# Retention state updates in four row groups of 32 tokens, and four feed-forward weight blocks in two column parts

## The chip, the cores and the metric

The kernel runs on one core of one Trainium2 chip, in one launch. The metric is the device time of that launch in microseconds (us). Before the change it is 1624.82 us, the median of 3 runs (1624.66 to 1625.16). TensorE (PE) does the matrix products, VectorE (DVE), ScalarE (ACT) and GpSimd (POOL) the rest, and SyncE (SP) issues nearly all of the DMA transfers.

## The reference

One layer of a hybrid decoder, for 256 prompt tokens and 8 sample sequences of 8 tokens (320 tokens in all), with a model width of 2048:

```
mod = silu(c) @ w_ada + b_ada                      # six modulation vectors per sequence
h   = rmsnorm(x, g_pre_mix) * (1 + sc1) + sh1
q, k, v, g, u, vs = split(h @ w_in)                # 48 tiles of 128 features
q, k = rotary(q), rotary(k) * 128 ** -0.5
o, S = retention(q, k, v, s0)                      # 8 heads of 128
m   = concat(silu(g) * layernorm(o), gelu(u) * spatial_gate(layernorm(gelu(vs)))) @ w_o
x   = x + gt1 * rmsnorm(m, g_post_mix)
f   = square(relu((rmsnorm(x, g_pre_ffn) * (1 + sc2) + sh2) @ w_ff1)) @ w_ff2
x   = x + gt2 * rmsnorm(f, g_post_ffn)
```

In the retention, each head of each sample sequence has a state of 128 x 128, and the layer returns the new one: `S_new = S * gamma**8 + sum over the 8 tokens of gamma**(7-s) * k_s^T v_s`. That is 8 heads x 8 sequences = 64 products over 8 tokens each.

## The kernel before

Features lie on the partitions and the 320 tokens on the free axis. Each weight block of 128 x 128 is split into a high and a low part (ACT's cast at L234, DVE's subtraction at L110), each activation tile too, and a product is three matmuls of 320 columns into one accumulator: high x high, high x low, low x high (`mm3`, L243 to L245). These 9216 matmuls are the bulk of PE's work; below they are the main matmuls. Weights come in pieces of 1 MB through four raw buffers; the adaLN weights (`adaw`) share those buffers, and their small matmuls (L187, here "ada rows", four of which run in the four column groups of the array) are strewn between the others.

The input projection runs over K in slices of 1, 1, 2, 4 and 8 blocks. In the last slice (8 blocks, 24 main matmuls per tile of 128 features) the finished tiles go straight into the mixers: after tile 7 the spatial gate's norm (`sgu`), and after every sixth tile from 13 on one call of `ret_pair` for two heads (four calls, here the first to the fourth pair). Such a call does, for each of its two heads: rotary on q and k (`rot`: four ACT copies into `sw` and six DVE products and sums), transposes of v and k on PE (`pv`, `pk`, L412 to L420), scores (`sc`, L426 to L428), masked scores on DVE (`sT`, `s_pad`, with the mask `dm` loaded by DMA at L406), and outputs (`po`, L437 to L444, the last eight of which read the old states `s0`, loaded at L404). The sample tokens of the two heads lie on partitions 0 to 63 and 64 to 127 of `vts` and `kts`.

Then, once per pair, the state update: POOL makes, for two sequences at a time, `ve`, a copy of `vts` for each of the two in which the rows of other sequences are zero and the others carry the decay (`bm` holds these factors); PE multiplies `kts` with it, one product of 64 rows and 256 columns per head (`pn`, L465, from the pool of three small PSUM buffers); DVE adds the result to the decayed old state (L470) and SP stores it (L471).

The order of instructions on each engine is not the source's. The framework's scheduler orders them by source position and by its own estimate of when operands and buffers come free, so work of the next tiles is placed between the steps of a pair where it fits. Each engine then runs its list strictly in that order, and so does SP with the DMA issues. PSUM has eight buffers of one bank: four accumulators (`new_acc`), three small ones (`small`) and one for the ada rows. `NSLOT` is the number of SBUF slots of 128 x 320 from which nearly all tiles come, `ve` among them.

Of the kernel before, what the change touches and what calls it, by code (L numbers as in the profile page):

```python
# [26 lines left out]
EPS = 1e-6  # L27
NSLOT = 104
NRAW = 4
# [23 lines left out]
def _per_piece(ci):  # L53
    """Column tiles in a piece of w_in for slice ci of K."""
    return 8 if ci == 0 else 16 // CHUNKS[ci]


def _w_in_pieces():
    """Pieces of w_in in load order: (K blocks, column tiles)."""
    out, k0 = [], 0  # L60
    for ci, kc in enumerate(CHUNKS):
        nt = _per_piece(ci)
        for q in range(0, ZT, nt):
            out.append((list(range(k0, k0 + kc)), N_ORDER[q : q + nt]))
        k0 += kc
    return out + [(list(range(KB)), [t]) for t in G_ORDER]


def _ada_groups():
    """Groups of w_ada columns (feature tiles of 128) in load order, by the part that they serve."""  # L70
    pre, k0 = [], 0
    for kc in CHUNKS:
        if kc == 1:
            pre.append([KB + k0, k0])
        else:
            pre += [[KB + k, KB + k + 1, k, k + 1] for k in range(k0, k0 + kc, 2)]
        k0 += kc
    gt1 = [[2 * KB + 4 * q + j for j in range(4)] for q in range(4)]
    ffn = [[4 * KB + k, 4 * KB + k + 1, 3 * KB + k, 3 * KB + k + 1] for k in range(0, KB, 2)]
    gt2 = [[5 * KB + 4 * q + j for j in range(4)] for q in range(4)]  # L80
    return pre, gt1, ffn, gt2
# [3 lines left out]
def hybrid_step(ctx: ExitStack, tc, A, O):  # L85
# [15 lines left out]
    def slot(s="z", dt=F32, shape=(P, T)):  # L101
        return slots.tile(list(shape), dt, tag="slot", name=nm(s))
# [14 lines left out]

# [1 line left out]
    eps = cp.tile([P, 1], F32, name="eps")  # L119
# [16 lines left out]
    crs = cst[:, 288:352].rearrange("p (h s) -> p h s", h=H)  # L136
    bm = cst[:, 352:384].rearrange("p (q b) -> p q b", q=4)
    bada = vec[:, 0:96]
# [10 lines left out]
    def rsqrt_(out, var, n):  # L149
        """out = 1/sqrt(var + EPS); var [P, n]."""  # L150
        y, a = [slot("rq") if n == T else tp.tile([P, n], F32, tag=f"rq{n}", name=nm("rq")) for _ in range(2)]
        S.activation(y, var, AF.Abs_reciprocal_sqrt, bias=eps)
        V.scalar_tensor_tensor(out=a, in0=y, scalar=-0.5, in1=y, op0=ALU.mult, op1=ALU.mult)
        V.scalar_tensor_tensor(out=a, in0=var, scalar=EPS, in1=a, op0=ALU.add, op1=ALU.mult)
        V.scalar_tensor_tensor(out=out, in0=a, scalar=1.5, in1=y, op0=ALU.add, op1=ALU.mult)
# [4 lines left out]
    def mean_rsqrt(parts, pm=None):  # L160
        """[P, T] squares (any number of parts) -> 1/sqrt(mean + EPS) on every partition."""
        if pm is None:
# [6 lines left out]

# [1 line left out]
    ada_piece = [0]  # L171

    def ada_group(feats):
        """Generator: one step per 1 MB piece; feats are feature tiles 0..95."""
        ncol = P * len(feats)
# [46 lines left out]

# [1 line left out]
    def load_w(src, ncol=KB, eng=None):  # L224
        """A piece of ncol 128x128 blocks; returns the (high, low) pair of each block."""
        w = wp.tile([P, 2048], F32, tag="raw", bufs=NRAW, name=nm("raw"))
# [13 lines left out]
    def mm3(acc, w, a, start, stop):  # L240
# [4 lines left out]
        PE.matmul(acc[:, :T], wl, ah, start=False, stop=stop)  # L245

    def new_acc():
        return ps_acc.tile([P, 512], F32, tag="acc", name=nm("acc"))
# [7 lines left out]
    def modulate(xt, r, Am, Sm, f, eng=None):  # L256
        """xt*A*r + shift, as a high and a low part; A and shift per feature and sequence."""
        t = slot("mt")
# [12 lines left out]

# [1 line left out]
    k0s = [sum(CHUNKS[:i]) for i in range(len(CHUNKS))]  # L273
# [20 lines left out]

# [1 line left out]
    gateT = [None] * 8  # L296
# [72 lines left out]

# [1 line left out]
    def rot(q):  # L371
# [7 lines left out]
    oT = [None] * 8  # L379
    # sample tokens on partitions: sequence b = 4i + j, step s at row 32j + 8i + s, other rows zero  # L380
    q_pad = [cp.tile([P, 272], F32, name=f"q_pad{i}") for i in range(2)]
# [10 lines left out]
    def ret_pair(qkv, pr, o, mv):  # L392
        """Heads 2*pr and 2*pr+1: scores, states, token-major outputs and their statistics."""
        kts, vts = slot("kts"), slot("vts")
        os_ = slot("os")
        s0s, qs = [], []
        for e in range(2):
# [59 lines left out]
            s0s.append(s0)  # L457
        for i in range(4):
            ve = slot("ve")
            tt(ve[:, :256].rearrange("p (b e) -> p b e", b=2), vts[:, :128].unsqueeze(1).broadcast_to([P, 2, P]),  # L460
               bm[:, pr, 2 * i : 2 * i + 2].unsqueeze(2).broadcast_to([P, 2, P]), ALU.mult, G)
            pns = [small("pn") for _ in range(2)]
            for e in range(2):
                rw = slice(64 * e, 64 * e + 64)
                PE.matmul(pns[e][:, :256], kts[rw, :128], ve[rw, :256], start=True, stop=True)  # L465
            for e in range(2):
                h = 2 * pr + e
                g8 = float((1.0 - 2.0 ** (-5.0 - h)) ** NS)
                sb = s0s[e][i][:, :256]
                V.scalar_tensor_tensor(out=sb, in0=sb, scalar=g8, in1=pns[e][:, :256], op0=ALU.mult, op1=ALU.add)  # L470
                nc.sync.dma_start(O["ss"][h, i], sb)  # L471
        return os_
# [27 lines left out]

# [1 line left out]
    z = {}  # L502
# [82 lines left out]

# [1 line left out]
    for gi, f in enumerate(G_ORDER):  # L587
# [7 lines left out]

# [1 line left out]
    def project(name, base, n, act, order, first4, extra, done, w0=None):  # L597
        """n tiles of 128 outputs, contraction over act; done(m, acc) takes each."""
        m = 0
        while m < n:  # L600
# [16 lines left out]
            for i in range(KB):  # L617
                k = order[i]
                mm3(acc, w[k], act[k], i == 0, i == KB - 1)
            done(m, acc)  # L620
# [6 lines left out]
    def add_sq(key, src, final):  # L627
        """Squares of a tile; all but the final one are summed first."""
        sq = slot("sq")
# [22 lines left out]
    project("w_o", 0, KB, mix, ks_o, True, lambda: steps(ada_b, EXTRA_O), done_o)  # L652
# [1 line left out]
    w0 = load_w(A["w_ff1"][0])  # L654
# [23 lines left out]

# [1 line left out]
    facc = [None] * KB  # L680
# [31 lines left out]
def _consts():  # L712
# [27 lines left out]
    for pr in range(4):  # L740
        for b in range(NB):
            for e in range(2):
                col = np.where(sb == b, gam[2 * pr + e] ** (NS - 1.0 - ss), 0.0) * sc
                cst[64 * e : 64 * e + 64, 352 + 8 * pr + b] = col

# [90 lines left out]
```

## Time and profile before

| | |
|---|---|
| median of 3 runs | 1624.82 us |
| profiled execution: span | 1622.0 us |
| profiled execution's own time beside its span | the page gives the span only; the median of the runs lies 2.8 us above it |
| PE busy | 1567.2 us, 97% of the span |
| DVE busy | 822.3 us, 51% |
| ACT busy | 577.3 us, 36% |
| POOL busy | 260.8 us, 16% |
| four pairs of `ret_pair` | between about 262 and 417 us from the start |

A busy share is an average over stages. A row of the timeline gives the start, the length, the engine, the line and operation, what is written from what, and in brackets the engine's idle time just before with what ended it. `x16` stands for 16 instructions in one row. A float32 product takes two passes through the array, so it shows as two matmuls and two weight loads.

### The profile page before, as it was taken

Reading aid. Unit: us, or ns where it says so; the run is one execution under the profiler, and the core shown is the slowest. Engines: PE = TensorE matmul, PEld = TensorE weight load, DVE = VectorE, ACT = ScalarE, POOL = GpSimd, SP = SyncE. Lnnn points to the kernel's source line nnn. Section 1 sums busy time; section 2 is a strip of 40 time slices with the busy share of each in tenths; the row PEclk is TensorE's granted clock in tenths of the full one; section 3 lists DMA queues with packets and bytes.
Section 4 is the critical chain, followed back from the end, with each engine's and each line's share of the span. In section 5 each row is a group of like instructions: output and inputs, shape, how many; then the busy total and the mean of one; then the engine's idle time right before and its main releaser. Section 6 shows DMA issues by size and latency. Waiting matters only on the chain.

```text
span 1622.0 us, 25797 instructions
## 1 busy us (share of the span) xinstructions
PE 1567.2 (97%) x10744; PEld 1437.5 (89%) x10744; DVE 822.3 (51%) x1306; ACT 577.3 (36%) x847; POOL 260.8 (16%) x287
## 2 busy tenths in 40 slices
PE   4999998999999999899999999999999999999994
PEld 3788887888788888588899999999999999999994
DVE  5676658576744444863433344444444444444455
ACT  3523234233433323343333334332344323343331
POOL 2510016000000111621100022100121000211222
PEclk8999999999999999999999999999999999999997
DMA  6777785556566776766644444443444344444421
GB/s 244 282 290 300 314 321 194 199 212 228 203 253 256 284 278 257 278 244 249 253 155 156 145 143 155 156 148 140 155 156 150 140 152 157 154 139 150 156 104 65
DMA packets 63620, 325.03 MB, mean 200 GB/s; under 512 B 7152, under 2 KB 26096, under 8 KB 27024
## 3 DMA queue, kind: packets, MB, share of 16 engines
q1 hardware_dynamic: 61680, 320.89, 53.6%
q8 instruction: 84, 1.38, 0.4%
q10 hardware_dynamic: 1584, 1.68, 0.3%
q0 software_dynamic: 240, 0.82, 0.1%
q14 instruction: 32, 0.26, 0.0%
HBM read 315.76 MB, written 7.60 MB: 199 GB/s over the span
## 4 chain that ended last, share of the span: by engine, by line
PE 92%; DVE 5%; ACT 1%; DMA 1%; issue 1%; POOL 0%; SPq 0%; DVEq 0%; POOLq 0%
PE acc L243 28%; PE acc L245 27%; PE acc L244 27%; PE ada L187 6%; DVE gm L110 1%; PE pm L158 1%; DVE z L110 1%; PE pn L465 1%; DVE wl L110 1%; DVE gv L346 1%; DMA x<-in_x_dram 0%; DMA adaw<-in_w_ada_dram 0%; DVE x L110 0%; PE gate L361 0%; PE adaT L202 0%
## 5 line engine op out<-in xcount | busy, mean ns | idle before, releaser
L243 PE MATMUL acc<-hi,wh 128*128 128x320 f32 x3072 | 957.9, 313 | 9.6 <-ACT hi L266 6.6
L245 PE MATMUL acc<-hi,wl 128*128 128x320 f32 x3072 | 953.1, 310 | 1.2 <-DVE wl L110 1.2
L244 PE MATMUL acc<-lo,wh 128*128 128x320 f32 x3072 | 952.3, 310 | 1.8 <-DVE lo L110 1.5
L110 DVE TENSOR_TENSOR wl<-raw,wh 128x1024 fp32r<-128x1024 f32 x381 | 468.5, 1230 | 516.5 <-ACT wh L234 515.4
L234 ACT CAST wh<-raw 128x1024 fp32r<-128x1024 f32 x384 | 402.0, 1047 | 745.4 <-PE acc L244 709.7
L243 PEld LDWEIGHTS acc<-hi,wh 128*128 128x128 f32 x3072 | 577.6, 188 | 74.0 <-issue 32.0
L244 PEld LDWEIGHTS acc<-lo,wh 128*128 128x128 f32 x3072 | 578.7, 188 | 5.3 <-DVE lo L110 3.9
L245 PEld LDWEIGHTS acc<-hi,wl 128*128 128x128 f32 x3072 | 578.6, 188 | 3.6 <-issue 1.6
L110 POOL TENSOR_TENSOR a<-rl 128x320 f32<-128x320 f32 x64 | 89.0, 1391 | 705.2 <-ACT rl L686 705.2
L187 PE MATMUL ada<-adaw,csil 128*32 128x512 f32 (+1 forms) x800 | 108.3, 594 | 1.2 <-DMA adaw<-in_w_ada_dram 1.2
L110 DVE TENSOR_TENSOR z<-z,acc 128x320 f32<-128x320 f32 x140 | 66.4, 484 | 62.1 <-PE acc L245 61.6
L110 POOL TENSOR_TENSOR sq<-sq,sq 128x320 f32<-128x320 f32 x28 | 40.6, 1448 | 292.1 <-ACT sq L630 292.0
L110 DVE TENSOR_TENSOR lo<-a,hi 128x320 fp32r<-128x320 f32 x64 | 32.6, 509 | 64.7 <-ACT hi L252 64.7
L252 ACT CAST hi<-a 128x320 fp32r<-128x320 f32 x64 | 29.4, 459 | 94.4 <-POOL a L110 94.4
L110 DVE TENSOR_TENSOR f<-f,acc 128x320 f32<-128x320 f32 x48 | 23.4, 488 | 69.3 <-PE acc L245 69.3
L187 PEld LDWEIGHTS ada<-adaw,csil 128*32 128x32 f32 x800 | 19.2, 109 | 30.5 <-issue 26.6
L110 POOL TENSOR_TENSOR mt<-mt,A 128x64 f32<-128x64 f32 x31 | 14.8, 477 | 139.5 <-DVE A L212 115.5
L110 POOL TENSOR_TENSOR ve<-vts,cst 128x256 f32<-128x256 f32 x16 | 12.6, 814 | 114.1 <-PE pk L420 64.5
L686 ACT ACTIVATE rl<-acc 128x320 f32<-128x320 f32 x64 | 27.5, 430 | 2.4 <-PE acc L245 2.4
L265 ACT ACTIVATE hi<-mt,SH 128x256 fp32r<-128x256 f32 x32 | 16.2, 507 | 19.5 <-DVE mt L259 19.5
L110 POOL TENSOR_TENSOR z<-z,zt 128x320 f32<-128x320 f32 x20 | 21.1, 1090 | 5.6 <-ACT zt L579 5.5
L198 DVE STREAM_TRANSPOSE part<-ada 128x512 f32<-128x512 f32 (+1 forms) x25 | 17.2, 689 | 7.2 <-PE ada L187 7.1
(147 smaller groups left out, 631.3 us busy)
## 6 DMA issues: line engine op xcount, KB each, us to landing
raw<-in_w_ff_dram SPq DMA_DIRECT2D x128, 1024.0 KB, 4.8
adaw<-in_w_ada_dram SPq DMA_DIRECT2D x96, 1024.0 KB, 5.2
raw<-in_w_in_dram SPq DMA_DIRECT2D x45, 1024.0 KB, 4.9
raw<-in_w_o_dram SPq DMA_DIRECT2D x16, 1024.0 KB, 4.8
x<-in_x_dram SPq DMA_DIRECT2D x27, 160.0 KB, 5.9
s<-in_s_dram SPq DMA_DIRECT2D x32, 128.0 KB, 4.8
out_ss_dram<-s SPq DMA_DIRECT2D x32, 128.0 KB, 1.8
raw<-in_w_in_dram SPq DMA_DIRECT2D x6, 512.0 KB, 4.5
```

Source lines behind the costliest of these rows:

```text
L110: (eng or V).tensor_tensor(out=out, in0=a, in1=b, op=op)
L158: PE.matmul(pm[:, :T], ones, q, start=first, stop=last)
L187: PE.matmul(acc[32 * j : 32 * j + 32, :ncol], csil[:, kb, :], w[:, k * ncol : (k + 1) * ncol], start=kb < 4, stop=kb >= KB - 4, tile_posit ...
L198: V.transpose(part[:, :ncol], acc[:, :ncol])
L234: S.copy(wh[:, :n], r)
L243: PE.matmul(acc[:, :T], wh, ah, start=start, stop=False)
L244: PE.matmul(acc[:, :T], wh, al, start=False, stop=False)
L245: PE.matmul(acc[:, :T], wl, ah, start=False, stop=stop)
L252: S.copy(hi, src)
L346: V.tensor_scalar(g, g, mv[:n, t, 0:1], rs[:n, t : t + 1], op0=ALU.subtract, op1=ALU.mult)
L465: PE.matmul(pns[e][:, :256], kts[rw, :128], ve[rw, :256], start=True, stop=True)
L686: S.activation(rl, acc[:, :T], AF.Relu)
```

## The change

`ret_pair` makes one `ve` per pair, for four sequences at once (512 columns), in a buffer of its own. A product now takes 32 rows of `kts` (four sequences of one head) and 512 columns, so there are four per pair, each in its own group of 32 rows of the array. Their results go into two small PSUM buffers and two accumulators, alternately. DVE's eight additions and the eight stores per pair are of the same shape as before. `bm` shrinks from eight factors per pair to four. In the feed-forward part, blocks 4 to 7 of tile 8 of the first slice of `w_ff1` are multiplied by the 256 prompt columns and the 64 sample columns apart, six matmuls in place of three. `NSLOT` goes from 104 to 105. The diff's other lines only drop comments.

```diff
-NSLOT = 104
+NSLOT = 105
...
-    bm = cst[:, 352:384].rearrange("p (q b) -> p q b", q=4)
+    bm = cst[:, 352:368].rearrange("p (q j) -> p q j", q=4)
...
+    def mm3_two(acc, w, a):
+
+        for c in (slice(0, TP), slice(TP, T)):
+            for wi, ai in ((0, 0), (0, 1), (1, 0)):
+                PE.matmul(acc[:, c], w[wi], a[ai][:, c], start=False, stop=False)
...
-        for i in range(4):
-            ve = slot("ve")
-            tt(ve[:, :256].rearrange("p (b e) -> p b e", b=2), vts[:, :128].unsqueeze(1).broadcast_to([P, 2, P]),
-               bm[:, pr, 2 * i : 2 * i + 2].unsqueeze(2).broadcast_to([P, 2, P]), ALU.mult, G)
-            pns = [small("pn") for _ in range(2)]
-            for e in range(2):
-                rw = slice(64 * e, 64 * e + 64)
-                PE.matmul(pns[e][:, :256], kts[rw, :128], ve[rw, :256], start=True, stop=True)
-            for e in range(2):
-                h = 2 * pr + e
-                g8 = float((1.0 - 2.0 ** (-5.0 - h)) ** NS)
-                sb = s0s[e][i][:, :256]
-                V.scalar_tensor_tensor(out=sb, in0=sb, scalar=g8, in1=pns[e][:, :256], op0=ALU.mult, op1=ALU.add)
-                nc.sync.dma_start(O["ss"][h, i], sb)
+        ve = wp.tile([P, 4, P], F32, tag="ve", bufs=1, name=nm("ve"))
+        tt(ve, vts[:, :128].unsqueeze(1).broadcast_to([P, 4, P]), bm[:, pr, :].unsqueeze(2).broadcast_to([P, 4, P]), ALU.mult, G)
+        pns = [new_acc() if g % 2 else small("pn") for g in range(4)]
+        for g in range(4):
+            rg = slice(32 * g, 32 * g + 32)
+            PE.matmul(pns[g][:, :512], kts[rg, :128], ve[rg].rearrange("p j e -> p (j e)"), start=True, stop=True, tile_position=(32 * g, 0))
+        for g in range(4):
+            e, i = divmod(g, 2)
+            h = 2 * pr + e
+            g8 = float((1.0 - 2.0 ** (-5.0 - h)) ** NS)
+            for u in range(2):
+                sb = s0s[e][2 * i + u][:, :256]
+                V.scalar_tensor_tensor(out=sb, in0=sb, scalar=g8, in1=pns[g][:, 256 * u : 256 * u + 256], op0=ALU.mult, op1=ALU.add)
+                nc.sync.dma_start(O["ss"][h, 2 * i + u], sb)
...
-                mm3(acc, w[k], act[k], i == 0, i == KB - 1)
+                if first4 and m == 8 and 4 <= i < 8 and name == "w_ff1":
+                    mm3_two(acc, w[k], act[k])
+                else:
+                    mm3(acc, w[k], act[k], i == 0, i == KB - 1)
```

The order of the instructions moves in the four pairs. PE in the third pair, before: the end of the first head's `po`, the second head's transposes of v (`pv`), and the next tile's main matmuls (`acc`).

```order
L444 MATMUL po_3842<-s_760_3810,q_pad_215 32x128 x2
L412 MATMUL pv_3887<-cst,z_423 128x128 x2
L413 MATMUL pv_3887<-cst,z_423 128x128
L243 MATMUL acc_3991<-hi_2175,wh_3977 128x320
L244 MATMUL acc_3991<-lo_2176,wh_3977 128x320
L245 MATMUL acc_3991<-hi_2175,wl_3978 128x320
```

The same place on PE in the changed kernel, as far as the first state product (`acc<-ve`); `ada` are ada rows, `pk` and `sc` the second head's transposes of k and its scores.

```order
L450 MATMUL po_3814<-s_746_3782,q_pad_215 32x128 x2
L418 MATMUL pv_3859<-cst,z_423 128x128 x2
L419 MATMUL pv_3859<-cst,z_423 128x128
L187 MATMUL ada_3638<-adaw_4011,csil 32x512 x3
L425 MATMUL pk_3866<-cst,z_417 128x128 x2
L426 MATMUL pk_3866<-cst,z_417 128x128
L432 MATMUL sc_3874<-z_405,z_417 128x256
L433 MATMUL sc_3874<-z_405,z_417 128x128
L434 MATMUL sc_3874<-z_405,z_417 128x64
L187 MATMUL ada_4370<-adaw_4368,csil 32x512
L470 MATMUL acc_3910<-ve_3907,kts_3764 128x512
```

Before, 25 main matmuls stood between `pv` and `pk`, and from the pair's first `pv` to its last `pn` there were 41, 48, 41 and 41 in the four pairs. Now there is none in any of them: the next tile's main matmuls begin behind the last state product. Ada rows stand there instead: 7, 4, 3 and 4 between `pv` and `pk`, and 12, 8, 9 and 11 in a whole pair, where it was 4, 0, 4 and 4. The two state products that go to accumulators take them ahead of the next tile's in the list. On DVE the instructions from the `po` copies' statistics to the second head's rotary stand as before.

SP's list in the third pair, before: the next weights (`raw`), the second head's old states (`s`) and mask (`dm`), then an ada piece.

```order
L227 DMA raw_4414<-in_w_in_dram 128x2048
L404 DMA s_774_3877<-in_s_dram 128x256
L404 DMA s_775_3878<-in_s_dram 128x256
L404 DMA s_776_3879<-in_s_dram 128x256
L404 DMA s_777_3880<-in_s_dram 128x256
L406 DMA dm_3885<-in_dmask_dram 128x320
L180 DMA adaw_4424<-in_w_ada_dram 128x2048
```

And in the changed kernel.

```order
L227 DMA raw_4358<-in_w_in_dram 128x2048
L180 DMA adaw_4368<-in_w_ada_dram 128x2048
L410 DMA s_760_3849<-in_s_dram 128x256
L410 DMA s_761_3850<-in_s_dram 128x256
L410 DMA s_762_3851<-in_s_dram 128x256
L410 DMA s_763_3852<-in_s_dram 128x256
L412 DMA dm_3857<-in_dmask_dram 128x320
```

The ada piece went ahead of the states and the mask; its raw buffer is the one that the three ada rows behind `pv` read last. In the first pair a `raw` piece moved likewise, behind the same kind of ada rows; in the second and fourth pair the piece ahead takes a buffer that is free before `po`.

## Rows read from the trace of the kernel before

**Rows 1.** The page, busy time: us, share of the span, instructions.

```profile
PE 1567.2 (97%) x10744; PEld 1437.5 (89%) x10744; DVE 822.3 (51%) x1306; ACT 577.3 (36%) x847; POOL 260.8 (16%) x287
```

**Rows 2.** The page, chain that ended last, by engine.

```profile
PE 92%; DVE 5%; ACT 1%; DMA 1%; issue 1%; POOL 0%; SPq 0%; DVEq 0%; POOLq 0%
```

**Rows 3.** Groups by shape: busy us, mean ns of one, idle before and its releasers.

```profile
L187 PE MATMUL ada<-adaw,csil 128*32 128x512 f32 x736 | 101.6, 606 | 0.0
...
L465 PE MATMUL pn<-ve,kts 64*128 64x256 f32 x64 | 14.0, 418 | 0.5 <-DVE s L470 0.2
L110 POOL TENSOR_TENSOR ve<-vts,cst 128x256 f32<-128x256 f32 x16 | 12.6, 814 | 114.1 <-PE pk L420 64.5 <-DVE vts L416 40.5 <-ACT kts L424 9.1
L470 DVE SCALAR_TENSOR_TENSOR s<-s,pn 128x256 f32<-128x256 f32 x32 | 12.5, 415 | 0.6
...
L465 PEld LDWEIGHTS pn<-ve,kts 64*128 64x128 f32 x64 | 8.5, 185 | 5.2 <-issue 2.4 <-DVE s L470 2.1
```

**Rows 4.** Timeline, third pair: start us, length us, engine, line, operation.

```profile
364.05 1.06 PE L187 MATMUL ada<-adaw,csil 128*32 128x512 f32 x8
...
365.56 2.20 SPq L404 DMA_DIRECT2D s<-in_s_dram  x4
365.59 0.38 PE L437 MATMUL po<-vt,sT 128*128 128x128 f32 x2
...
367.34 0.44 PE L412 MATMUL pv<-cst,z 128*128 128x128 f32 x2
367.48 0.37 ACT L448 COPY o<-po 128x256 f32<-128x256 f32 x1 [3.32 <-PE po L444]
...
369.00 0.49 DVE L110 TENSOR_TENSOR z<-z,cos 128x320 f32<-128x320 f32 x1 [0.16 <-ACT sw L374]
...
371.30 0.48 DVE L110 TENSOR_TENSOR z<-z,sw 128x320 f32<-128x320 f32 x1
...
371.93 0.41 PE L419 MATMUL pk<-cst,z 128*128 128x128 f32 x2 [0.38 <-DVE z L110]
372.13 0.29 DVE L416 COPY vts<-pv 64x128 f32<-64x128 f32 x1
...
372.59 3.31 POOL L110 TENSOR_TENSOR ve<-vts,cst 128x256 f32<-128x256 f32 x4 [32.73 <-PE pk L420]
...
372.94 0.33 PE L428 MATMUL sc<-z,z 128*128 128x64 f32 x2
...
377.17 3.63 PE L465 MATMUL pn<-ve,kts 64*128 64x256 f32 x16
```

**Rows 5.** Timeline, first pair, PE alone.

```profile
269.74 0.41 PE L245 MATMUL acc<-hi,wl 128*128 128x320 f32 x1 [1.17 <-DVE wl L110]
...
283.31 0.80 PE L437 MATMUL po<-vt,sT 128*128 128x128 f32 x2 [2.87 <-DVE sT L110]
...
286.62 0.69 PE L412 MATMUL pv<-cst,z 128*128 128x128 f32 x2
...
288.39 0.47 PE L244 MATMUL acc<-lo,wh 128*128 128x320 f32 x1
288.65 0.47 PE L245 MATMUL acc<-hi,wl 128*128 128x320 f32 x1
...
290.76 0.31 PE L245 MATMUL acc<-hi,wl 128*128 128x320 f32 x1
290.91 0.31 PE L243 MATMUL acc<-hi,wh 128*128 128x320 f32 x1
...
292.26 0.60 PE L426 MATMUL sc<-z,z 128*128 128x256 f32 x2
292.70 0.38 PE L427 MATMUL sc<-z,z 128*128 128x128 f32 x2
```

**Rows 6.** Stretches of 10 us: busy time of PE, PEld, DVE, ACT, POOL; granted clock; DMA share; GB/s.

```profile
275.00:285.00 10.00, 6.84 (x42) 5.03 (x41) 8.58 (x13) 1.81 (x4) 9.22 (x9) 0.88 0.56 220
285.00:295.00 10.00, 10.00 (x69) 9.31 (x70) 6.80 (x20) 4.26 (x10) 1.61 (x3) 0.78 0.47 169
```

**Rows 7.** DMA issues: count, KB each, median us from issue to landing.

```profile
adaw<-in_w_ada_dram SPq DMA_DIRECT2D x96, 1024.0 KB, 5.2
...
s<-in_s_dram SPq DMA_DIRECT2D x32, 128.0 KB, 4.8
...
dm<-in_dmask_dram SPq DMA_DIRECT2D x8, 160.0 KB, 4.5
```

More of the change, by code (lines that the diff above doesn't have):

```diff
@@ L740, in _consts @@
     for pr in range(4):
-        for b in range(NB):
+        for j in range(4):
             for e in range(2):
-                col = np.where(sb == b, gam[2 * pr + e] ** (NS - 1.0 - ss), 0.0) * sc
-                cst[64 * e : 64 * e + 64, 352 + 8 * pr + b] = col
+                col = np.where(sb % 4 == j, gam[2 * pr + e] ** (NS - 1.0 - ss), 0.0) * sc
+                cst[64 * e : 64 * e + 64, 352 + 4 * pr + j] = col
     tri = np.zeros((P, 192))
```

## The prediction, written before the changed kernel ran

> **What bounds the kernel now.** I read the busy times first: PE is busy for 1567.2 of 1622.0 us [rows 1], and the chain of waits, followed back from the end, runs 92% through PE [rows 2]. So the kernel is PE's list, worked off in order: what PE has to do, plus the time in which its next instruction waits. A gain elsewhere counts only if PE waits for it, and a new wait on PE costs its whole length, since everything behind it in PE's list is late by as much. Then I read the groups by shape for the state update [rows 3], and the timeline of the third pair for what surrounds it [rows 4].
>
> There the reader is to see three things. The sixteen passes of the old state products hold PE for 3.63 us (377.17 on). They are float32 passes of 256 columns, and they go through three small PSUM buffers that DVE empties by eight additions of 0.415 us each [rows 3]: 8 x 0.415 = 3.3 us, so DVE paces them more than PE's own work does. Second, the second head's `pk` starts at 371.93 after a wait of 0.38 us for DVE's `z`, that is 4.59 us behind `pv` (367.34) [rows 4]. Behind `po` stand a copy on ACT, statistics on DVE, four ACT copies and seven DVE operations of the rotary, and they run without a pause from 369.00 to 371.78. Third, PE filled these 4.59 us with 25 main matmuls, which by their starts at full clock take 0.147 us each (290.76 to 290.91) [rows 5]: 3.7 us of work that had to be done anyway.
>
> **The change, part by part.** All sums are made against the profiled execution; the runs' median lies 2.8 us above its span, and I add that at the end.
>
> *A, the state products.* Four float32 products per pair of 512 columns, so eight passes, into four buffers that need not be emptied in between. Two passes of 256 columns take 0.44 us where nothing holds them (292.26 to 292.70) [rows 5], so a pass of 512 takes 0.44. One after the other: 8 x 0.44 = 3.5 us per pair. All four at once, as the ada rows do in the four column groups: eight passes of 512 in 1.06 us [rows 4]. But the order splits them, two ahead of `po` and two behind it (one and three in the third pair), so at most two or three run beside each other; halfway between is the case of two at a time, some 2.6 us with the fill. I take 2.6, a gain of 4 x (3.63 - 2.6) = 4.1, between 0.5 and 10.3. DVE's additions remain, beside PE.
>
> The trace shows no 32-row group, only the four column groups above. [...] I keep the middle, because the order doesn't let the four follow each other.
>
> *B, the wait for the rotary.* In the changed order nothing of the main matmuls stands between `pv` and `pk`, while the chain from `po` to `pk` is the same instructions on ACT and DVE. PE has only `pv` (0.3 us) and 3 ada rows in the third pair, 4 in the second and fourth, 7 in the first; four take 1.0 us [rows 4]. The third pair then waits 4.59 - 0.3 - 0.75 = 3.5, the second and fourth 4.6 - 0.3 - 1.0 = 3.3 each. In the first pair PE comes from a wait at half clock (below), so `pv` and seven ada rows, most of them at half rate, fill about 3.6, and 1.0 remains. Together 11.1, less the 0.38 and about as much in two other pairs that PE already waits there: +10.1. The ada rows are only moved, so they cost nothing here and are missing nowhere else. The bounds are 9 to 12, because ACT and DVE are unchanged. Behind the waiting `pk` in PE's list stand the scores, all state products and then the whole rest of the input projection.
>
> *C, the wait for `ve`.* POOL starts on `ve` 0.66 us behind `pk` (372.59), as soon as DVE has written `vts`. 512 columns are two of the old ones, 2 x 0.814 = 1.6 us [rows 3], so the first state product can start 2.3 us behind `pk`. PE is through with the scores 1.2 us behind it (372.94 and 0.2). Before, ten main matmuls and `po` lay in between; now nothing does (in the third pair an ada row). That is 1.1 us in three pairs and some 0.3 in the third: +3.6. Below, 2 if POOL is quicker while DVE rests; above, 5.
>
> *D, one more switch.* The products enter and leave twice per pair. PE's weight loads show 2.4 us of "issue" idle at L465 in all [rows 3], some 0.2 per entry in twelve; four more entries: +0.8, at most 1.6. [...]
>
> *E, late loads.* In the first and third pair, SP now holds the second head's old states and mask behind a 1 MB piece whose buffer comes free only when the ada rows behind `pv` are done, about 1.4 us after `po`. Four state loads, 2.2 us of issuing [rows 4], and the mask follow, so the mask is issued some 3.9 us after `po` and lands 4.5 later [rows 7], at 8.4. `pk` is at 4.6, its scores end at 5.8, and DVE's `sT` wants the mask at 6.0; but `po` could not start before the first state products are done, at about 8.2, and needs `sT` 0.6 earlier. What is left is about 0.8 plus what the 1 MB ahead takes from the DMA engines, less what it lands early: I take 1.0 in two pairs, +2.0, from 0 to 5.
>
> *F, the clock.* In the first pair PE waited 2.87 us, and the rows behind it are at half rate: main matmuls 0.26 us apart (288.39 to 288.65), and `po` up to `pv` took 3.31 us (283.31 to 286.62) against 1.75 in the third pair (365.59 to 367.34). [...] A wait of 1.17 us (269.74) was followed by a full-rate row [rows 5]. The new waits of 3.3 to 3.5 us are longer than the one that did it. If it comes, `pk`, scores, products and `po` lose about 1.2 + 1.6, less the 1.1 of C that now is work: 1.7 per pair. I count it in two of three pairs: 3.4. The first pair gives back the 0.9 that eight slow main matmuls lost. Net +2.5, from -0.9 to +9.
>
> *G, the feed-forward blocks.* Twelve main matmuls become 24, of 256 and 64 columns. If time went by columns it would be 0. If a 64-column matmul cost as much as a whole one, because its weights are loaded anew, 12 x 0.147 = 1.8. I take 0.8. `NSLOT`, the smaller `bm` and POOL's shorter list (16 to 4 instructions) cost nothing: nothing on PE waits for them.
>
> Sum: -4.1 + 10.1 + 3.6 + 0.8 + 2.0 + 2.5 + 0.8 = +15.7. So 1622.0 + 15.7 + 2.8 = 1640.5 us.
>
> **The rivals.**
>
> *R1, faster:* the four products run all at once, and the chain from `po` to `pk` shortens, because DVE has fewer tasks while no tile is being finished. With a chain of 2.5 us, B is 1.4 + 1.2 + 1.2 + 0, less 1.0 that was there: +2.8. A is -10.3, C 2, D and G 0.8 each: -3.9, or 1620.9 us. It decides as soon as B and C together are under about 8.7. Against it: the chain's rows follow each other without a gap [rows 4], with no other work between them that could go. For it: nothing but A's lower end.
>
> *R2, no change:* A at its best with the row groups side by side in spite of the split, the clock stays up, the loads are in time: -10.3 + 9.0 + 2.0 + 0 + 0 - 0.9 + 0 = -0.2, or 1624.6. Each end alone is possible, all of them together hardly.
>
> *R3, slower than forecast:* the loads decide. With the mask 2.5 us late in two pairs (E 5) and the lower clock in every pair up to the main matmuls (F 9), the sum is +25.2, or 1650 us. For it speaks that SP's list is in order and that the new wait is longer than the one that lowered the clock; against it, that B's wait gives the DMA time to land.
>
> *R4, the change moves nothing:* excluded for the waits, since the order shows no main matmul inside a pair; only their lengths are open.
>
> **How the numbers follow.** The forecast gets 0.73 with its own range of 1630 to 1648, R3 0.12, R2 0.07, R1 0.08. A measurement of this kernel tells 0.2%, 3.2 us, from no change. R1 is faster, R2 the same, the others slower: 0.08, 0.07, 0.85. The range leaves out R1, R2 and the far end of R3: 1629 to 1652. The predicted time is the forecast's 1640.5.
>
> **What would show it.** In the changed profile's timeline: PE's `pk` of the second head with an idle of about 3.4 us for DVE's `z` in three pairs and less in the first (B); the first state product idle for POOL's `ve` by about 1 us (C); products of some 1.3 us per two in place of one block of 3.63 (A); the mask's landing in the first and third pair against `sT` (E); a granted clock below 1 in more stretches between 280 and 430 us than before (F); 64-column matmuls with their spacing in the first `w_ff1` slice (G). PE's busy time hardly changes, and the span grows by its idle time. It is wrong if `pk` waits under 2 us in the later pairs, or if the state products alone give back more than 10 us. Outside these four pairs and the four feed-forward blocks nothing should move.

## The result, and the profile after

The changed kernel takes 1651.28 us (median of 4 runs, 1647.33 to 1654.81) against 1624.74 beside it: ratio 1.0169, interval 1.0153 to 1.0185, or +26.5 us. The forecast was 1640.5, so the direction was right and the size too small by 11. The profiled execution has a span of 1652.4 us, 30.4 more than before; the mean granted clock is 0.971 in it. Two of the four runs have 0.976 and spans of 1645.6 and 1646.6, so some of the loss comes and goes with the clock.

The page first: PE is busy 18 us longer than in [rows 1], with almost as many instructions; the chain stays on PE as in [rows 2].

```profile
PE 1585.2 (96%) x10724; PEld 1445.8 (87%) x10724; DVE 821.4 (50%) x1306; ACT 577.3 (35%) x847; POOL 252.0 (15%) x275
...
PE 92%; DVE 5%; DMA 1%; ACT 1%; POOL 0%; issue 0%; SPq 0%; ACTq 0%; DVEq 0%; POOLq 0%
```

So most of the loss is not idle time: the same rows take longer. The waits of PE in the stretch of the four pairs (260 to 460 us; total, times, longest):

```profile
PE pk L425 <- DVE z L110: 8.6, 5, 3.5
PE po L443 <- DVE sT L110: 4.9, 2, 2.7
PE ada L187 <- DMA adaw<-in_w_ada_dram: 1.7, 1, 1.7
PE acc L470 <- POOL ve L110: 1.3, 2, 0.9
...
```

With 1.2 for `wl` it is 17.7 us, where before had 5.5 (2.87 and 1.17 of it in [rows 5], 0.38 in [rows 4]): 12.2 more. The rest is in the clock. Stretches of 10 us of the changed kernel (PE busy, granted clock, DMA share, GB/s), to be read against [rows 6]:

```profile
295.00:305.00 10.00, 9.60 (x44) 0.50 0.47 170
...
345.00:355.00 10.00, 10.00 (x54) 0.60 0.31 105
...
385.00:395.00 10.00, 10.00 (x40) 0.50 0.31 105
...
435.00:445.00 10.00, 10.00 (x47) 0.50 0.32 106
```

Read in stretches of 1 us, the granted clock is 0.50 from 282 to 288 and from 295 to 305 us around the first pair, from 343 to 353 in the second, from 384 to 400 in the third and from 429 to 445 in the fourth, and 1.00 between them except for the stretch in which it changes (0.54 to 0.98). So it is at half rate for 10 to 17 us around each pair, and PE is busy for most of them. PE in the second pair, where [rows 4] show the same work of another pair before:

```profile
336.79 0.44 PE L418 MATMUL pv<-cst,z 128*128 128x128 f32 x2
...
341.37 0.41 PE L425 MATMUL pk<-cst,z 128*128 128x128 f32 x2 [3.04 <-DVE z L110]
...
343.13 2.08 PE L470 MATMUL acc<-ve,kts 32*128 32x512 f32 x4 [0.42 <-POOL ve L110]
345.14 0.80 PE L443 MATMUL po<-vt,sT 128*128 128x128 f32 x2
...
348.45 2.08 PE L470 MATMUL pn<-ve,kts 32*128 32x512 f32 x4
350.46 0.64 PE L243 MATMUL acc<-hi,wh 128*128 128x320 f32 x1
350.89 0.47 PE L244 MATMUL acc<-lo,wh 128*128 128x320 f32 x1
```

The wait for z is there with 3.04 us. Behind it the first two products take 2.01 us, `po` 3.31 (1.75 in [rows 4]), the other two products 2.01, and the main matmuls start 0.27 us apart in place of 0.147, eight of them here (the first, behind the products, is followed after 0.43). In the third pair the low clock is there from the waiting `pk` on, in the fourth from the ada rows ahead of it (0.54 from 428 to 429), and in both it lasts through 15 main matmuls at the end. The fourth pair, PE:

```profile
427.51 1.42 PE L187 MATMUL ada<-adaw,csil 128*32 128x512 f32 x8 [1.66 <-DMA adaw<-in_w_ada_dram]
429.89 0.66 PE L425 MATMUL pk<-cst,z 128*128 128x128 f32 x2 [0.96 <-DVE z L110]
...
439.62 0.64 PE L243 MATMUL acc<-hi,wh 128*128 128x320 f32 x1
...
444.06 0.47 PE L244 MATMUL acc<-lo,wh 128*128 128x320 f32 x1
```

From 429.89 to 444.06, 14.2 us, PE has no gap that the profile shows, and the granted clock of the whole stretch is 0.50.

In the feed-forward part the four two-part blocks stand in one row of 24 (PE, one block and the first matmul of the next):

```profile
776.91 0.28 PE L251 MATMUL acc<-hi,wh 128*128 128x256 f32 x1
...
777.27 0.20 PE L251 MATMUL acc<-hi,wh 128*128 128x64 f32 x1
777.30 0.28 PE L251 MATMUL acc<-lo,wh 128*128 128x64 f32 x1
777.41 0.28 PE L251 MATMUL acc<-hi,wl 128*128 128x64 f32 x1
777.52 0.36 PE L251 MATMUL acc<-hi,wh 128*128 128x256 f32 x1
```

A block takes 0.69 us where three main matmuls take 3 x 0.147 = 0.44. The first 64-column matmul is 0.03 us ahead of the next, the other two 0.11, nearly as much as the 0.12 of a 256-column one, and 0.08 more go to the change back (777.52 to 777.72).

### The profile page after: what moved, and what is told of

Read it like the earlier page. It is cut to its first block, busy times and chain, and to the rows that moved or that the text cites. A ratio compares the mean times of both kernels' runs of the same rounds, so it can differ in the third digit from the quotient of the medians.

```text
span 1652.4 us, 25752 instructions
## 1 busy us (share of the span) xinstructions
PE 1585.2 (96%) x10724; PEld 1445.8 (87%) x10724; DVE 821.4 (50%) x1306; ACT 577.3 (35%) x847; POOL 252.0 (15%) x275
## 4 chain that ended last, share of the span: by engine, by line
PE 92%; DVE 5%; DMA 1%; ACT 1%; POOL 0%; issue 0%; SPq 0%; ACTq 0%; DVEq 0%; POOLq 0%
PE acc L243 28%; PE acc L245 27%; PE acc L244 27%; PE ada L187 5%; DVE gm L110 1%; PE pm L158 1%; DVE z L110 1%; DVE gv L352 1%; DVE wl L110 1%; PE pn L470 0%; PE po L450 0%; DMA adaw<-in_w_ada_dram 0%; DMA cst<-in_cst_dram 0%; PE acc L470 0%; DVE x L110 0%; PE po L443 0%
## 5 line engine op out<-in xcount | busy, mean ns | idle before, releaser
L110 POOL TENSOR_TENSOR mt<-mt,A 128x64 f32<-128x64 f32 x31 | 14.5, 467 | 138.3 <-DVE A L212 114.8
L110 POOL TENSOR_TENSOR ve<-vts,cst 128x512 f32<-128x512 f32 x4 | 4.2, 1039 | 144.7 <-DVE vts L422 94.6
```

What stands on the lines that cost most here:

```text
L110: (eng or V).tensor_tensor(out=out, in0=a, in1=b, op=op)
```

## The experiments

The theory: products two and four draw from the accumulators, and with that the main matmuls leave the pairs; the waits follow, and from the waits the low clock. The rival: the 32-row products themselves cost the time. All times are medians, each beside the kernel before on the same chip (1624.04 for the first four, 1623.61 for the fifth to eighth, 1623.37 and 1622.97 for the last two pairs).

**1. The four products without an accumulator.**

```diff
-        pns = [new_acc() if g % 2 else small("pn") for g in range(4)]
+        pns = [small("pn") for g in range(4)]
```

> The changed kernel, but all four state products take a small PSUM buffer (three there are), none an accumulator. The order then has 37, 44, 37 and 37 main matmuls inside the four pairs again, where the changed kernel has none and the kernel before 40, 44, 40 and 40. Theory P (the accumulators drawn for two products drive the main matmuls out of the pairs; the waits and the lower clock follow from that): 1619 us, 1615 to 1623: the kernel before, less some 6.5 for shorter products (two of them 1.13 us at full clock), plus 1.0 for the feed-forward blocks; granted clock as before, waits of PE in the pairs under 6 us. Rival S (the 32-row groups and their mode switches themselves cost the time and the clock): 1640 or more.

1628.85 us, ratio 1.0030 (1.0020 to 1.0041). In the trace 38, 45, 38 and 38 main matmuls stand between a pair's first `pv` and its last `pn` again (41, 48, 41 and 41 before, none in the changed kernel). With them 22 of the 26.5 us are gone: the order made the loss. But the gain of 6.5 did not come either, and the time lies above theory P's range. PE behind `po` of the third pair:

```profile
377.24 1.85 PE L470 MATMUL pn<-ve,kts 32*128 32x512 f32 x6
379.60 1.09 PE L470 MATMUL pn<-ve,kts 32*128 32x512 f32 x2 [0.51 <-DVE s L477]
380.62 0.63 PE L245 MATMUL acc<-hi,wl 128*128 128x320 f32 x1
381.05 0.47 PE L243 MATMUL acc<-hi,wh 128*128 128x320 f32 x1
```

The fourth product waits for one of the three buffers and then takes 1.02 us alone, so the block is 3.38 us long against 3.63 in [rows 4]. Behind it the clock is low again: the main matmuls of 381.05 and after are at half rate, 0.27 us apart, and so they are behind the first and the fourth pair, but not behind the second.

**2. The old products with an accumulator.**

```diff
-            pns = [small("pn") for _ in range(2)]
+            pns = [small("pn"), new_acc()]
```

> The kernel before with its two row groups of 64, one change: the second state product of each two takes an accumulator in place of a small buffer. The order then has no main matmul inside the pairs. Theory P: 1649 us, 1642 to 1656, with waits of about 3 us of pk for DVE's z and half rate behind them, though there is no 32-row group in it. Rival S: 1625 us, 1622 to 1628.

1643.98 us, ratio 1.0121 (1.0105 to 1.0136): +20 without a single 32-row product. The wait for z in the second pair is 3.04 us, as in the changed kernel. It is 5 us less than forecast but in theory P's range, and the clock comes back earlier than in the changed kernel (0.69 from 345 to 355 us, where it is 0.60 there), which goes the same way. In the second pair it is back at the end of the product block, before the main matmuls:

```profile
342.57 0.41 PE L419 MATMUL pk<-cst,z 128*128 128x128 f32 x2 [3.04 <-DVE z L110]
...
350.89 0.56 PE L465 MATMUL pn<-ve,kts 64*128 64x256 f32 x1
...
351.64 0.31 PE L244 MATMUL acc<-lo,wh 128*128 128x320 f32 x1
```

**3. The wait filled with work.**

```diff
             pk = small("pk")
+            for _ in range(22 if e == 1 else 0):
+                PE.matmul(pk[:, :T], hx[0][0][:, :P], hx[0][0], start=True, stop=True)
```

> The changed kernel with 22 more matmuls of the main matmuls' form (their results are overwritten) between pv and pk of the second head of each pair; they lie in the wait for z. They do no useful work, so the wait is not won back. Theory W (the wait of about 3 us lowers the clock, and the lower clock costs some 15 to 20 us behind it): 1635 us, 1630 to 1641, granted clock near 1 in the second to fourth pair. Rival V (the clock falls by other things: the late mask, the few rows of the state products, po): 1648 to 1654, half rate still there.

1633.98 us, ratio 1.0065 (1.0052 to 1.0077), 16.6 us less lost than in the changed kernel, though PE has 88 matmuls more (13 us). The granted clock is 1.00 behind every pair (ahead of the first pair's end it is 0.86); behind the third:

```profile
385.00:395.00 10.00, 10.00 (x76) 1.00 0.65 224
```

So with work in the wait the low clock (0.50 from 385 to 395 in the changed kernel) is gone: in these pairs the idle time brings it on, and theory W holds. At full clock the products can be read too, third pair:

```profile
378.44 1.12 PE L472 MATMUL acc<-ve,kts 32*128 32x512 f32 x2 [0.16 <-POOL ve L110]
379.49 0.49 PE L445 MATMUL po<-vt,sT 128*128 128x128 f32 x2
...
381.34 0.70 PE L472 MATMUL pn<-ve,kts 32*128 32x512 f32 x2
...
382.41 0.41 PE L243 MATMUL acc<-hi,wh 128*128 128x320 f32 x1
```

One product takes 1.05 us, three take 1.07: here a block has one price, whatever is in it. No product in it waits for a buffer; where one does, this is not so (twelfth experiment).

**4. Loads at the start of the pair.**

```diff
...
+        s0d, dms = [], []
+        for e in range(2):
+            s0d.append([slot("s0") for _ in range(4)])
+            for i in range(4):
+                nc.sync.dma_start(s0d[e][i][:, :256], A["s0"][2 * pr + e, i])
+            dms.append(slot("dm"))
+            nc.sync.dma_start(dms[e], A["dmask"][2 * pr + e])
...
-            s0 = [slot("s0") for _ in range(4)]
-            for i in range(4):
-                nc.sync.dma_start(s0[i][:, :256], A["s0"][h, i])
-            dm = slot("dm")
-            nc.sync.dma_start(dm, A["dmask"][h])
+            s0, dm = s0d[e], dms[e]
...
```

> The changed kernel with the old states and masks of both heads loaded at the start of the pair, ahead of the large pieces in SP's queue. Theory E1 (late loads cost what the waits of po and sT show): the 2.27 us of po in the first pair go, with about 0.5 elsewhere: 1648.5 us, 1646 to 1650, clock unchanged. Rival E2 (the late loads prolong the time at low clock): 1640 to 1645. Rival E3 (hidden): 1650.5 to 1653.

1653.12 us, ratio 1.0177 (1.0157 to 1.0198): as the changed kernel. It does not settle the price of the late loads. The wait of `po` in the first pair is gone, but the first head's `pk` now waits 5.56 us for z in the same pair (no more than 0.3 before), so one wait took the other's place.

**5. Three products in place of four, in the first experiment's kernel.** The edit is shown against the changed kernel. The additions of the fourth product are left out with it, so two states of each pair get no sum.

```diff
...
-        pns = [new_acc() if g % 2 else small("pn") for g in range(4)]
-        for g in range(4):
+        pns = [small("pn") for g in range(3)]
+        for g in range(3):
...
-                V.scalar_tensor_tensor(out=sb, in0=sb, scalar=g8, in1=pns[g][:, 256 * u : 256 * u + 256], op0=ALU.mult, op1=ALU.add)
+                if g < 3:
+                    V.scalar_tensor_tensor(out=sb, in0=sb, scalar=g8, in1=pns[g][:, 256 * u : 256 * u + 256], op0=ALU.mult, op1=ALU.add)
...
```

> The first experiment's kernel (all products from the small buffers, main matmuls back in the pairs) without the fourth state product of each pair: the last two states of the second head are left out of the sum. Theory L (the fourth product, which waits 0.51 us for a buffer and then takes 1.02 us alone, costs its own time and lowers the clock behind it in two pairs): 1628.9 - 4 x 1.5 - 3 = 1620 us, 1617 to 1622, clock 1.00 behind the third and fourth pair. Rival M (the 32-row products themselves lower the clock): 1622.5 to 1625, clock 0.9 there as before.

1619.29 us, ratio 0.9975 (0.9965 to 0.9984). Against the kernel before it is 4.3 faster where the first experiment was 4.8 slower: 9.1 us. The fourth product's own time, wait and all, is 4 x 1.53 = 6.1, so 3.0 remain for the clock. It is 1.00 behind the third pair, as it is behind the first and the fourth:

```profile
375.00:390.00 15.00, 15.00 (x104) 1.00 0.81 282
```

In the first experiment the like stretch, and those behind the first and the fourth pair, are at 0.89:

```profile
380.00:395.00 15.00, 15.00 (x95) 0.89 0.75 244
```

Three such stretches lose 3 x 15 x 0.11 = 5 us in that execution, so the remainder of 3.0 is only a rough price. Theory L holds: a wait of 0.51 us and one product alone behind it were enough in three of the four pairs. Which of the two it was is not shown, since both went together.

**6. Old products, wait filled.** The second experiment's kernel with the third one's lines.

> The second experiment's kernel (old products in two row groups, one of each two in an accumulator) with the same 22 added matmuls in the wait for z as in the third. Against the third, both at full clock, this is the price of the row groups alone. Theory G (at full clock the four groups gain: two blocks of some 1.1 us in place of one of 3.63): 1634.0 - 1.0 for the feed-forward blocks + 5.5 = 1638.5 us, 1636.5 to 1641. Rival N (the four groups gain nothing even there): 1632 to 1634.

1633.14 us, ratio 1.0061 (1.0048 to 1.0074): 9.5 above the kernel before, where the third experiment is 9.9 above it. The third has 1.0 for the feed-forward blocks in it, and both have a median granted clock of 0.988. So at the same clock the row groups win some 0.6 us in four pairs, less than the intervals are wide: rival N. What I had missed is that the accumulator frees the old products as well. Their block in the second pair:

```profile
339.77 0.48 PE L467 MATMUL pn<-ve,kts 64*128 64x256 f32 x1
...
342.37 0.41 PE L243 MATMUL acc<-hi,wh 128*128 128x320 f32 x1
```

2.6 us with a wait of 0.40 in it, in place of 3.63: it was the three buffers that paced them, and two blocks of 1.05 are little better.

The two runs also show that not every wait lowers the clock. In the profiled executions both kernels wait 2.67 us for `sT` in the first pair. The last sixteen passes of the `po` behind it take 1.08 us in the third experiment (from 285.14), which is half rate, and 0.65 in the sixth (from 284.92).

**7. Fourteen times as many two-part blocks, in the kernel before.**

```diff
...
-                mm3(acc, w[k], act[k], i == 0, i == KB - 1)
+                if first4 and 8 <= m < 12 and 1 <= i < 15 and name == "w_ff1":
+                    mm3_two(acc, w[k], act[k])
+                else:
+                    mm3(acc, w[k], act[k], i == 0, i == KB - 1)
...
```

> The kernel before with 56 of the two-part blocks in w_ff1 (14 of each of the tiles 8 to 11) in place of the change's 4. Theory: a block costs what the four took in the changed kernel's trace, 0.69 us in place of 0.44, so 56 x 0.25 = 14: 1638 us, 1636 to 1641. Rival by columns: 1624. Rival by the whole price of a main matmul for each 64-column one: 56 x 0.44 = 24.7: 1649.

1637.05 us, ratio 1.0083 (1.0069 to 1.0097): 13.4 / 56 = 0.24 us a block, or 1.0 for the change's four.

**8. The four products of the second pair 17 times over.**

```diff
-        for g in range(4):
+        for g in [g for _ in range(17 if pr == 1 else 1) for g in range(4)]:
```

> The changed kernel with the four state products of the second pair issued 17 times over (the same result each time), 16 rounds of four more than it has. It is read in the rows for what a round of four takes. Theory Q (four row groups run beside each other, as three did in 1.07 us in the third experiment): 0.9 to 1.1 us a round at full clock, twice that at half. Rival T (two at a time, as the forecast took): 1.8 to 2.2 at full clock. Rival U (one after the other): 3.5.

The time of 1662.4 us is a single run and isn't used; the rows are. PE in the second pair, two of the buffers (the accumulators' rows lie between):

```profile
350.89 1.06 PE L470 MATMUL pn<-ve,kts 32*128 32x512 f32 x2
...
352.60 1.06 PE L470 MATMUL pn<-ve,kts 32*128 32x512 f32 x2
...
354.08 0.59 PE L470 MATMUL pn<-ve,kts 32*128 32x512 f32 x2
...
364.81 0.59 PE L470 MATMUL pn<-ve,kts 32*128 32x512 f32 x2
```

At full clock four passes start every 0.43 us (354.08 to 364.81 in 25 steps), so a round of four products, eight passes (the changed kernel's 16 products show as 32 matmuls), takes 0.86: theory Q. At half clock it is 1.71 (350.89 to 352.60). The 3.5 us of the serial estimate, over 0.86, is 4.1: here four groups run fully beside each other once they follow without a gap.

**9 and 10. Four small buffers, three accumulators**, for the first experiment's kernel with whole feed-forward blocks, and for the kernel before.

```diff
-    ps_acc = ctx.enter_context(tc.tile_pool(name="ps_acc", bufs=4, space=bass.MemoryType.PSUM))
+    ps_acc = ctx.enter_context(tc.tile_pool(name="ps_acc", bufs=3, space=bass.MemoryType.PSUM))
...
-    ps_sm = ctx.enter_context(tc.tile_pool(name="ps_sm", bufs=3, space=bass.MemoryType.PSUM))
+    ps_sm = ctx.enter_context(tc.tile_pool(name="ps_sm", bufs=4, space=bass.MemoryType.PSUM))
...
-                accs = [new_acc() for _ in range(4)]
+                accs = [new_acc() for _ in range(3)] + [small("acc")]
```

> The first experiment's kernel (all four state products from the small buffers, main matmuls in the pairs) with four small buffers and three accumulators in place of three and four (the fourth accumulator of a first group of tiles is a small buffer), and the feed-forward blocks whole. Theory X (in the first experiment the fourth product's wait and the 1.02 us that it takes alone cost some 1.5 us a pair and the clock; with a buffer of its own it runs beside the others, in one block of some 1.8 us in place of the 3.63 of before): 1616 us, 1613 to 1620. Rival Y (what the four groups gain is lost again elsewhere, with three accumulators for the main matmuls): 1623 to 1628.

> The kernel before with four small buffers and three accumulators, the control for the ninth experiment: all else as before. Theory X: the old products are less held up by the three buffers: their block of 3.63 us falls to some 3.2, four times: 1622 us, 1620 to 1624. Rival Y (three accumulators hold up the main matmuls): 1626 or more. Rival Z (the buffers alone give all of the gain): 1616 to 1619.

1631.99 us (ratio 1.0052, 1.0039 to 1.0064) and 1631.23 (1.0051, 1.0037 to 1.0065): rival Y for the tenth, and the ninth is slower still than its rival Y (1623 to 1628). But the loss is not in the pairs. Two marks of ACT's list, ahead of the pairs and behind them, in the kernel before, and then in the tenth experiment:

```profile
255.21 0.30 ACT L152 ACTIVATE rq<-sgu_mv,eps 128x3 f32<-128x3 f32 x1
...
646.20 0.53 ACT L152 ACTIVATE rq<-pm,eps 128x320 f32<-128x320 f32 x1
```

```profile
265.49 0.30 ACT L152 ACTIVATE rq<-sgu_mv,eps 128x3 f32<-128x3 f32 x1
...
653.95 0.53 ACT L152 ACTIVATE rq<-pm,eps 128x320 f32<-128x320 f32 x1
```

10.3 us are lost ahead of 255 us, 2.5 won by 646 and 3.6 by the end; for the ninth the same marks are at 266.29 and 654.45: 11.1 lost, 2.8 won by 646. So by these marks four buffers help the old products and the new ones alike. In the ninth the product block is 1.78 us, yet part of that gain is given back: DVE, which still has all its additions and the norm to do, is behind, and `oT` waits for it:

```profile
350.00 1.85 PE L470 MATMUL pn<-ve,kts 32*128 32x512 f32 x8
351.78 0.42 PE L243 MATMUL acc<-hi,wh 128*128 128x320 f32 x1
...
356.51 0.30 PE L502 MATMUL oT<-cst,o 128*128 128x128 f32 x1 [0.93 <-DVE o L501]
```

**11 and 12. The fourth bank lent to the products in the last slice only** (`nacc[1]` is false there; `extra_bank` gives the one buffer of a pool of its own, by which the accumulators' pool is smaller), for the kernel before, as shown, and in the twelfth for the fourth product of the row groups.

```diff
...
+        nacc[0] += 1
+        if nacc[1] and nacc[0] % 4 == 0:
+            return extra_bank("acc")
         return ps_acc.tile([P, 512], F32, tag="acc", name=nm("acc"))
...
-            pns = [small("pn") for _ in range(2)]
+            pns = [small("pn"), extra_bank("pn") if i % 2 else small("pn")]
...
```

> The kernel before, four accumulators as before outside the last slice of the input projection; within that slice (where the pairs are) the fourth bank serves the second product of every other two, so that four small buffers take the old products. The tenth experiment lost 10.3 us ahead of the pairs with three accumulators and won 3.6 behind; here the loss should be missing. Theory B (it is the buffers that pace the old products): 1620 us, 1618.5 to 1621.5. Rival O (three accumulators cost as much inside the last slice): 1623 to 1627.

> The changed kernel's four row groups with the same extra bank for the fourth product, three small buffers for the others, the feed-forward blocks whole; main matmuls in the pairs. One product then stands ahead of po (it waits for ve), three behind it. Theory K (a block of products costs about 1.05 us however few are in it, so two blocks give away what the four groups win): 1620 to 1623 us, no faster than the eleventh by more than 1. Rival H (the four groups win over two at equal buffers): 1614 to 1618.

1620.48 us, ratio 0.9983 (0.9974 to 0.9992), and 1621.45, ratio 0.9991 (0.9982 to 1.0000): the times of theories B and K. The eleventh is faster than both kernels of this study, by 2.5 us against the one before; with the same buffers the four row groups add nothing. The old products in it, second pair, 2.92 us from the first to the next row of another kind:

```profile
340.32 1.14 PE L474 MATMUL pn<-ve,kts 64*128 64x256 f32 x8
341.65 1.66 PE L474 MATMUL pn<-ve,kts 64*128 64x256 f32 x8 [0.19 <-DVE mv L465]
343.24 0.64 PE L188 MATMUL ada<-adaw,csil 128*32 128x512 f32 x4
```

The reason that theory K gives does not hold, though. In the twelfth, one product ahead of `po` takes 1.02 us (336.59 to 337.61), but the three behind it take 1.81, not 1.05:

```profile
339.70 1.88 PE L479 MATMUL pn<-ve,kts 32*128 32x512 f32 x6
341.51 0.42 PE L244 MATMUL acc<-hi,wh 128*128 128x320 f32 x1
```

In the trace's records two of them start together and the third 0.76 us later, 0.06 after ACT has copied `po` out of its buffer (340.13 and 0.27). So it most likely waits for that buffer; no run tries it apart. In the fifth experiment three products take 1.78, and in the ninth four, with the last one as late. A pair's products thus take 2.83 us here against 2.92 in the eleventh, and the two runs do not price the row groups with every buffer free. The third and the sixth come nearest to that, with 0.6 us.

## Why the prediction was right in sign and short in size

The measured 1651.28 lies above the forecast's own range of 1630 to 1648. Step by step, forecast and then the profiled execution of the changed kernel:

- **B, the wait for the rotary: +10.1; measured +8.9.** The waits are 3.04 and 3.50 us (forecast 3.3 and 3.5), 0.81 in the first pair (1.0), and in the fourth 0.96 behind 1.66 for an ada piece that landed late (3.3 together). That is 10.2 in all with the 0.27 of a first head, less 1.3 that were there. This step held, and the second experiment shows its cause, the order, without the row groups.
- **C, the wait for `ve`: +3.6; measured +1.3.** POOL took 1.04 us for 512 columns, not 1.6, so 0.93 and 0.42 us were left. In the third and fourth pair the scores at half rate hid it altogether.
- **E, late loads: +2.0; measured +2.1**, 2.27 us in the first pair, less 0.2 at another `po`. In the third DVE did wait 2.90 us for the mask, but PE was busy with products until 390.98 and did not see it. So the sum came right by luck: 2.3 and nothing in place of 1.0 twice.
- **G, the two-part blocks: +0.8; measured +1.0**, by rows and by the seventh experiment.
- **A, the state products: -4.1; measured +0.7.** Two blocks per pair, 1.05 us each at full clock, would have been -6. But seven of the eight blocks ran at half clock with 2.0 us each; with 1.1 for the other that is 15.2 against 4 x 3.63 = 14.5. The size of a block was near, its clock wrong. Nor is the gain one of the row groups alone: sixth and eleventh experiment.
- **D, the switches: +0.8**; no run shows them apart. If they cost anything, the block's 1.05 us holds it: that is 0.2 above two passes of 0.43 (eighth experiment).
- **F, the clock: +2.5; measured about +15**, and this is the step that failed. Of it, `po` is 4 x 1.56 = 6.2 (two at half rate in the first pair, where one was before), `pk` and scores 2.4 in two pairs, 53 main matmuls at 0.267 less the eight of before 5.4, ada rows 0.9. With what A lost by it, the clock costs some 22 us in this execution. I had let the low clock begin in two of three pairs and end with `po`, and the sum has 1.2 for `pk` and scores and 1.6 for `po`, but nothing for the products, which it names (half rate cost them 7 x 0.96 = 6.7, counted under A); the rows show it in every pair, and reaching through both product blocks and up to 15 main matmuls. In the kernel before, the granted clock is 0.50 from 283 to 289 us, behind the first pair's wait of 2.87, and 1.00 from 290 to 460.

The measured terms come to 29 of the 30.4 us. The kernel also reached the first pair 1.5 us earlier than in the execution of before (ACT's mark at 253.71 against 255.21), so about 3 us stay unassigned. The third experiment gives the clock's part another way: of its 16.6 us, 2.1 and 0.7 are E and C, and its matmuls cost 2.8 more than the waits they filled, so about 16.6 is the clock at the medians.

Rival R3 named the right thing and the nearest time, 1650, but half of its reason was wrong: the loads cost 2, not 5, the clock more than its 9. R1 and R2 needed a shorter chain or a clock that stays up, and neither came. That no main matmul stands in a pair was the base of the argument, and the first two experiments show by what it came about: which pool the products take. Why a request to the accumulators holds the main matmuls back (they were taken to be served in program order) was argued, not tried.

What stays open: why the low clock lasted through the 32-row products in the changed kernel and ended inside the old ones in the second experiment. Both follow waits of the same length (3.04 us in the second pair). Nor is it known why a wait of 2.67 us lowered the clock in the third experiment and not in the sixth.

## What to carry to other kernels

A buffer drawn from another pool can move more work than the instruction it serves: look in the order at what leaves the place, before pricing the instruction. A new wait on PE that lowers the clock is priced with all that runs at the lower clock behind it, up to the first full-rate row; here that was more than the wait itself (about 15 us by F, against 8.9 by B). Before giving credit to a new form of an operation, give the old form the same buffers.

## What the hardware showed that I had not expected

- A block of 32-row products (float32, 512 columns) takes 1.05 us with one in it and 1.07 with three when no product waits for a buffer (third experiment); without a gap, four take 0.86 (eighth).
- 14.2 us of PE work without a gap (`pk`, scores, products, `po`, then 4.4 us of main matmuls) passed at a granted clock of 0.50 before the full rate came back (changed kernel, fourth pair). In the second pair it came back 9.9 us behind the first product (343.13 to 353.02), and no sooner with four products at a time in place of main matmuls: 9.9 us in the eighth experiment (343.71 to about 353.6).
- A wait of 0.51 us, with a lone product behind it, was followed by the low clock in three of four pairs (first experiment, 0.89 over the 15 us behind the product).
- A 64-column matmul behind another, each with its own 128 x 128 weights, takes 0.11 us at a granted clock of 1.00, against 0.12 for 256 columns.
